# Seven-product pairs: weight sums by two adding transfers and two VectorE additions, attention outputs by way of DRAM

## The chip, the cores and the metric

One NeuronCore of a Trainium2 chip runs the program. The metric is device time in microseconds (us). The engines are TensorE (PE; its weight loads are PEld), VectorE (DVE), ScalarE (ACT), GpSimd (POOL) and SyncE (SP, which here only starts transfers). Transfers between DRAM and SBUF are started from the queues of SP, POOL and ACT. "L145" is line 145 of the kernel.

## The reference

A sequence of 512 tokens with 2048 channels passes through two blocks, all in float32.

- First block, two layers: `h = rmsnorm(x)`, `proj = h @ w_in`; sliding-window attention of 16 heads gives `ya`, latent attention of 8 heads gives `yb`, each times `silu` of its gate; then `x = x + concat(ya, yb) @ w_out`. A final norm follows.
- Second block, one layer: `zin = rmsnorm(x) @ w_in2` is cut into q, k, v, g_attn, u, g_pool, m_attn, m_pool. Stick-breaking attention and a multi-window pool give two outputs, each times `silu` of a gate and then through an up-projection (`w_aup`, `w_pup`); `merged = sigmoid(m_attn) * y_attn + sigmoid(m_pool) * y_pool`, and `x + merged @ w_out2` is normed.

The columns m_attn and m_pool of `zin`, 2048 each, are 32 column tiles of 128. They are what the "pairs" compute.

## The kernel before

**Split matmuls.** Activations lie with channels on the partitions, as tiles of 128 x 512 (channels x tokens). A float32 product is done in three TensorE passes on two rounded halves of each operand: high x high, low x high, high x low. For activations, `split` (L134 ff.) makes the halves: a cast on ACT (names end in `h`), and the difference on DVE (`l`). For weights SP loads a raw tile of 128 x 1024 (`wr`, `w_raw`, L177 to L180), ACT casts `wh` (L209) and DVE subtracts `wl` (L210, recorded as L121). `next_w` makes two weights ahead of the one TensorE works on. There are three buffers for `wh` and for `wl` each; there are three for `wr` and two for `ws`, and a load into a `wr` buffer waits until the `wl` of the tile that it held is done.

**Queues.** Each engine works its own list in order. TensorE's order is as written; a scheduler orders the lists of DVE, ACT, POOL and SP. A load on SP that waits holds up all that stands behind it on SP.

**First block.** Per layer: input products, the side work of the two attentions (stepped forward between matmuls), and at the end the output projection: 16 column tiles j, each a sum over 16 chunks `y[0..15]`, in two halves u of 8 chunks (u=0: y0 to y7, u=1: y8 to y15). The first three tiles run as a group: u=0 for three tiles, then u=1 for three. `yget(c)` splits chunk c. Chunks 0 to 7 are split early (at input product `qa` i, chunk i), 8 to 15 where the output projection first asks for them. All `y` stay in SBUF tiles ("slots", 76 of 128 x 528).

**Pairs.** `run_pair` (L303 ff.) computes two column tiles by seven half-width products in place of eight: 16 pairs, seven products each, each product 8 chunks x 3 passes = 24 matmuls with 256 columns. The results gather in three PSUM tiles z, x, y; ACT copies `m5` from z (L320) and `m1` from x (L322) after the first and second product, and the fourth product, which writes x again, cannot start before `m1`. The weights of the products are, in order: a21+a22, a11, a21+a22+a11, a12, a11+a21, a21+a22+a11+a12, a22 (`pair_steps`, L182 to L204). The sum of products 1, 3 and 6 lives in one tile `ws`, that of product 5 in a `wr` tile. Every addition is an adding transfer on POOL's queue (L192), four in a pair, beside four plain loads by SP. An adding transfer into `ws` must wait until the weight that `ws` held has been split. `pair_out` and `gate_sigmoid` then make two gates `sga` per pair, and SP stores them to DRAM (`sgd`, L1136).

**After the pairs** come 16 rounds of `au` and `pu` (up-projections), which read the 16 tiles `ol` (`o_load`, L1085 to L1088), loaded at the end of the last pair, each split into `oNh` and `oNl`.

Of the kernel before, what the change touches and what calls it, by code (L numbers as in the profile page):

```python
# [35 lines left out]
POOL_W = (2, 4, 8, 16)  # L36

GRP = 3
NSLOT = 76
HN = S // 2  # L40
NSIDE = 3
TP_WAIT = 4000
# [54 lines left out]
def trunk_kernel(ctx, tc, xT, w_in, w_qkv, w_out, w_in2, w_pool, w_aup, w_pup, w_out2, metaT, vec, cst, outT):  # L97
# [22 lines left out]
    def tt(out, a, b, op):  # L120
        nc.vector.tensor_tensor(out, a, b, op)  # L121
# [52 lines left out]
    wq = deque()  # L174
    wready = deque()

    def w_raw(src, n, tag="wr", bufs=3):  # L177
        raw = wp.tile([P, WCOLS], F32, tag=tag, name=tag, bufs=bufs)[:, :n]
        nc.sync.dma_start(raw, src)
        return raw  # L180
# [5 lines left out]
    def pair_steps(a11, a12, a21, a22, n):  # L186


        st = {}

        def add(t, src):
            nc.gpsimd.dma_start(t, src, accum_op=ALU.add)  # L192
            return t

        def s1():
            st["s"] = w_raw(a21, n, "ws", 2)
            return add(st["s"], a22)

        def p11():
            st["r"] = w_raw(a11, n)  # L200
            return st["r"]

        return [s1, p11, lambda: add(st["s"], a11), lambda: w_raw(a12, n), lambda: add(st["r"], a21),
                lambda: add(st["s"], a12), lambda: w_raw(a22, n)]  # L204

    def load_w_split(raw, n):
        hi = wp.tile([P, WCOLS], F32R, tag="wh", name="wh")[:, :n]
# [199 lines left out]
        nc.sync.dma_start(diag_t, cst[:, C_DIAG:C_DIAG + S])  # L407

    xd = [tc.dram_tile([P, NC, S], F32, name=f"xd{i}") for i in range(2)]

    def split_g(x, g, name):
        hi = slot(name + "h", F32R)
# [30 lines left out]
    def swa_pair(i, qps, r, st, nsink, gate, ydst):  # L443
# [78 lines left out]
            nc.scalar.copy(y[on], o[kv][off])  # L522
            tt(y[on], o[kv][on], y[on], ALU.add)
        nc.gpsimd.tensor_tensor(y, y, gate.pop(("a", i)), ALU.mult)
        ydst[8 + i] = y

    def lora_norm(pss, gcol, name, res):

# [73 lines left out]
    def mla_head(h, pr, kr, gate, ydst):  # L602
        hh = h % 2
        qh, ql = pr["qn", hh]
        kh, kl = pr["kn", hh]
        qr = pr["qr", hh]
        krh, krl = kr
        nm = small.tile([P, 4], F32, tag="nm4", name="nm4")
        rs = small.tile([P, 4], F32, tag="rs4", name="rs4")
        pts = []  # L610
        for i in range(NB):
            n = (i + 1) * P
            sc = ps_at("msc")
            qs = slice(i * P, n)
            mm3(sc[:, :n], qh[:, qs], ql[:, qs], kh[:, :n], kl[:, :n], True, False)
            mm2(sc[:, :n], qr[:, qs], krh[:, :n], krl[:, :n], False, True)
            p = slot("mp")
            nc.vector.tensor_tensor_reduce(p[:, :n], sc[:, :n], diag_t[:, S - n:], -MLA_SCALE, 1e38, ALU.add, ALU.min,
                                           nm[:, i:i + 1])
            act(p[:, :n], p[:, :n], AF.Exp, bias=nm[:, i:i + 1], scale=-1.0, accum_out=rs[:, i:i + 1])  # L620
            nc.vector.reciprocal(rs[:, i:i + 1], rs[:, i:i + 1])
            nc.vector.tensor_tensor(p[:, :n], p[:, :n], rs[:, i:i + 1].to_broadcast([P, n]), ALU.mult)
            pts.append(p)
            yield 1200
        yield 2500
        o = ps_at("mo")
        todo = []

        def pv(js, offs, th, tl):
            for j in js:  # L630
                vh, vl = pr["v", j // 2]
                vs = slice((j % 2) * 256 + hh * P, (j % 2) * 256 + hh * P + P)
                cs = slice(offs[j], offs[j] + (NB - j) * P)
                mm3(o[:, j * P:], vh[:, vs], vl[:, vs], th[:, cs], tl[:, cs], j == 0, j == 2)

        for js in ((0,), (1, 3), (2,)):
            tp = ps_at("mtp")
            off = 0
            offs = {}
            for j in js:  # L640
                offs[j] = off
                for i in range(j, NB):
                    transp(tp[:, off:off + P], pts[i][:, j * P:(j + 1) * P])
                    off += P
            th = slot("mTh", F32R)
            tl = slot("mTl", F32R)
            split(tp[:, :off], "", hi=th[:, :off], lo=tl[:, :off])
            if todo:
                pv(*todo.pop())
            todo.append((js, offs, th, tl))  # L650
            yield TP_WAIT
        pv(*todo.pop())
        while ("b", h) not in gate:
            yield 500
        y = slot("yb")
        tt(y, o, gate.pop(("b", h)), ALU.mult)
        ydst[h] = y

    def grouped(w, t0, n):
        for u in range(2):  # L660
# [64 lines left out]
    def layer(lay, h, rd, x_src, x_dst):  # L725
# [12 lines left out]
        y = [None] * NC  # L738
        ys = [None] * NC

        def yget(c):
            if ys[c] is None:
                need(lambda: y[c] is not None)
                ys[c] = split(y[c], f"y{c}")
                y[c] = None
            return ys[c]

# [5 lines left out]
        for kind, i in SEQ1:  # L753
            if kind == "cq":
                if i == 0:
                    pss = run_gemm(2, 8, hget, group=GRP)
                    need(lambda: "r" in rd)
                    start_side(lora_norm([scaled("cq", ps) for ps in pss], V_QA_G + 3 * lay, "cqn", st))
            elif kind == "ckv":
                ckv.append(scaled("ckv"))  # L760
                if i == 1:
                    start_side(lora_norm(ckv, V_KV_G + 2 * lay, "ckvn", st))
            elif kind == "kr":
                kr = split(rope_of(scaled("krf"), "kr"), "krs")
            elif kind == "gb":
                gate["b", i] = gate_silu(run_gemm(2, 8, hget), rd["r"], "gb")
            elif kind == "pa":
                need(lambda: "cqn" in st and "ckvn" in st)
                proj[i] = {}
                mla_proj_a(st["cqn"], st["ckvn"], proj[i])  # L770
                tick()
            elif kind == "pb":
                mla_proj_b(st["cqn"], st["ckvn"], proj[i])
                tick()
            elif kind == "pc":
                pr = proj.pop(i)
                mla_proj_c(st["ckvn"], pr)
                for hh in range(2):
                    start_side(mla_head(2 * i + hh, pr, kr, gate, y), 6000 + 3000 * hh)
            elif kind == "ka":  # L780
                ka = scaled("kaf")
            elif kind == "va":
                start_side(swa_prep(ka, scaled("vaf"), st))
            elif kind == "qa":
                yget(i)
                start_side(swa_pair(i, run_gemm(2, 8, hget), rd["r"], st, nsink, gate, y))
            elif kind == "ga":
                gate["a", i] = gate_silu(run_gemm(2, 8, hget), rd["r"], "ga")

        sq = SumSq("x")  # L790
        if lay == 1:
# [303 lines left out]
    for kind, i in SEQ2:  # L1095
# [32 lines left out]
        elif kind in ("ma", "mp"):  # L1128
# [3 lines left out]
                need(lambda: len(done) == SB)  # L1132
                oo = [None] * (2 * SB)
            at = i + (0 if kind == "ma" else NC)
            for d, t in enumerate(pair_out(run_pair(tset, 8), sr)):
                nc.sync.dma_start(sgd[:, at + d, :], gate_sigmoid(t, "sg"))  # L1136
            if (kind, i) == ("mp", NC - 2):
                X2 = tset = None
                for c in range(2 * SB):
                    oo[c] = o_load(c)  # L1140
        elif kind == "au":
            ya = slot("ym")
            ga = sg_load(i)
# [180 lines left out]
```

## Time and profile before

| | us |
|---|---|
| median of 3 runs | 2794.11 (2786.51 to 2795.55) |
| profiled execution | 2791.94 |
| its span in the trace | 2790.2 |
| PE busy | 2693.0, 97% of the span |
| DVE busy | 1593.4, 57% |
| ACT busy | 1216.4, 44% |
| POOL busy | 459.4, 16% |

PE is busy nearly throughout, and the mean granted clock is 0.989 of full speed. The profile's second part cuts the span into 40 slices of 69.8 us; TensorE's share is 9 tenths or more in all but the first, slices 30 to 35 (2022.8 to 2441.2 us) and the last. A busy PE is not always PE at its full pace, because each record runs from a matmul's start to its modelled end and the records overlap: with 256 columns one takes 0.28 us, and the next starts 0.118 us after it.

### The profile page before, as it was taken

To read this page: it belongs to the slowest core of one execution; us is meant where nothing else is said; L and a number is where in the kernel's file an instruction comes from. 1 tells how busy PE (TensorE), PEld (TensorE's weight loads), DVE (VectorE), ACT (ScalarE), POOL (GpSimd) and SP (SyncE) were. 2 spreads that over 40 slices of the span, in tenths; PEclk is the share of its full clock that TensorE was granted. 3 is DMA by queue.
4 is the path that set the end of the run, shared out by engine and by line. 5 is a ranking of instruction groups with operands and counts; after the bars stand their busy time and mean duration, and the time that the engine had idled before them with its cause. 6 is when DMAs were issued, how large, how long until landed. Compare 5 with 4: busy or idle time off the path is not lost.

```text
span 2790.2 us, 37552 instructions
## 1 busy us (share of the span) xinstructions
PE 2693.0 (97%) x14809; PEld 2321.5 (83%) x14809; DVE 1593.4 (57%) x2399; ACT 1216.4 (44%) x2021; POOL 459.4 (16%) x369
## 2 busy tenths in 40 slices
PE   7999999999999999999999999999988888899997
PEld 5888888888888888888898889898888888688886
DVE  5767567644477667665644444565555555544445
ACT  4445456422345455543334433433345555422322
POOL 4011022111001102124201111112311111011111
PEclk9999999999999999999999999999999999899999
DMA  6222222344322222234422222233388888644334
GB/s 201 75 74 71 77 81 69 111 147 139 97 76 64 78 81 76 76 125 150 134 78 76 79 79 82 70 113 103 94 202 196 198 200 196 183 149 139 125 121 137
DMA packets 107009, 322.39 MB, mean 116 GB/s; under 512 B 11712, under 2 KB 16192, under 8 KB 106832
## 3 DMA queue, kind: packets, MB, share of 16 engines
q1 hardware_dynamic: 97232, 285.78, 32.6%
q0 software_dynamic: 9456, 34.14, 7.0%
q8 instruction: 116, 1.90, 0.3%
q14 instruction: 61, 0.50, 0.1%
q10 hardware_dynamic: 144, 0.07, 0.0%
HBM read 294.78 MB, written 25.17 MB: 115 GB/s over the span
## 4 chain that ended last, share of the span: by engine, by line
PE 77%; DMA 10%; DVE 4%; issue 4%; ACT 4%; POOL 2%; POOLq 0%; SPq 0%; DVEq 0%; ACTq 0%
PE mm L145 55%; DMA ws<-in_w_in 9%; PE mmA L145 5%; PE mmB L145 5%; ACT wh L209 2%; DVE wl L121 1%; PE msc L145 1%; PE qn L145 1%; PE sc L145 1%; PE o L145 1%; PE mo L145 1%; DMA wr<-in_w_in 1%; PE tp L149 1%; ACT sp L128 1%; PE kn L145 1%
## 5 line engine op out<-in xcount | busy, mean ns | idle before, releaser
L209 ACT CAST wh<-wr 128x1024 fp32r<-128x1024 f32 (+2 forms) x448 | 461.6, 1030 | 906.6 <-PE mm L145 616.3
L121 DVE TENSOR_TENSOR wl<-wr,wh 128x1024 fp32r<-128x1024 f32 (+2 forms) x448 | 580.2, 1298 | 316.4 <-ACT wh L209 301.1
L145 PE MATMUL mm<-hh,wh 128*128 128x512 f32 x1024 | 411.7, 402 | 6.6 <-ACT wh L209 6.4
L145 PE MATMUL mm<-hl,wh 128*128 128x512 f32 x1024 | 404.9, 395 | 2.2 <-DVE hl L124 2.2
L145 PE MATMUL mm<-hh,wl 128*128 128x512 f32 x1024 | 405.1, 396 | 0.8 <-DVE wl L121 0.8
L145 PEld LDWEIGHTS mm<-hh,wl 128*128 128x128 f32 x1024 | 193.4, 189 | 47.7 <-DVE wl L121 2.4
L145 PEld LDWEIGHTS mm<-hh,wh 128*128 128x128 f32 x1024 | 194.0, 189 | 42.8 <-ACT wh L209 6.8
L145 PEld LDWEIGHTS mm<-hl,wh 128*128 128x128 f32 x1024 | 194.1, 190 | 39.1 <-DVE hl L124 3.7
L145 PE MATMUL mm<-Xh,wh 128*128 128x512 f32 x384 | 152.6, 398 | 0.0
L145 PE MATMUL mm<-Xh,wl 128*128 128x512 f32 x384 | 151.2, 394 | 0.0
L145 PE MATMUL mm<-Xl,wh 128*128 128x512 f32 x384 | 150.7, 392 | 0.0
L121 DVE TENSOR_TENSOR wl<-ws,wh 128x1024 fp32r<-128x1024 f32 x48 | 59.1, 1231 | 110.5 <-ACT wh L209 109.4
L392 POOL TENSOR_TENSOR gag<-gag,gaa 128x512 f32<-128x512 f32 x24 | 35.5, 1479 | 471.9 <-ACT gaa L128 471.9
L145 PE MATMUL mmA<-Xh,wh 128*128 128x264 f32 x384 | 109.6, 285 | 0.0
L145 PE MATMUL mmB<-Xl,wh 128*128 128x264 f32 x384 | 109.4, 285 | 0.0
L145 PE MATMUL mmB<-Xh,wh 128*128 128x264 f32 x384 | 109.4, 285 | 0.0
L145 PE MATMUL mmA<-Xh,wl 128*128 128x264 f32 x384 | 109.2, 284 | 0.0
L145 PE MATMUL mmA<-Xl,wh 128*128 128x264 f32 x384 | 109.1, 284 | 0.0
L145 PE MATMUL mmB<-Xh,wl 128*128 128x264 f32 x384 | 109.0, 284 | 0.0
L209 ACT CAST wh<-ws 128x1024 fp32r<-128x1024 f32 x48 | 50.3, 1048 | 131.1 <-DMA ws<-in_w_in 104.9
L145 PE MATMUL x<-Xh,wh 128*128 128x256 f32 x256 | 74.7, 292 | 22.4 <-ACT m L322 22.4
L192 POOL DMA_DIRECT2D ws<-in_w_in x48 | 42.6, 968 | 311.9 <-DVE wl L121 220.6
(874 smaller groups left out, 7040.5 us busy)
## 6 DMA issues: line engine op xcount, KB each, us to landing
wr<-in_w_in SPq DMA_DIRECT2D x272, 512.0 KB, 3.7
wr<-in_w_out SPq DMA_DIRECT2D x100, 512.0 KB, 3.6
ws<-in_w_in POOLq DMA_DIRECT2D x48, 512.0 KB, 6.0
ws<-in_w_in SPq DMA_DIRECT2D x16, 512.0 KB, 4.0
xd<-xn SPq DMA_DIRECT2D x32, 256.0 KB, 2.0
wr<-in_w_in POOLq DMA_DIRECT2D x16, 512.0 KB, 8.1
sgd<-sga SPq DMA_DIRECT2D x32, 256.0 KB, 2.5
wr<-in_w_aup SPq DMA_DIRECT2D x16, 512.0 KB, 3.7
```

The source lines that it names most:

```text
L121: nc.vector.tensor_tensor(out, a, b, op)
L128: nc.scalar.activation(out, x, func, bias=bias, scale=scale)
L145: nc.tensor.matmul(out, a, b, start=start, stop=stop, skip_group_check=True)
L149: nc.tensor.transpose(out, x, ident)
L192: nc.gpsimd.dma_start(t, src, accum_op=ALU.add)
L209: nc.scalar.copy(hi, raw)
L392: nc.gpsimd.tensor_tensor(g, g, a, ALU.mult)
```

## The change

1. `pair_steps`: the sum for product 5 (a21+a11) gets a load and an adding transfer of its own (`summed`), so that a11 stays as loaded. The two later additions into `ws` (a11 before product 3, a12 before product 6) are `tensor_tensor` additions in place on VectorE (`plus`). A pair then has five plain loads by SP and two adding transfers by POOL.
2. `wr` has four buffers, the slots are 74.
3. In the first block, chunks 0 to 13 of `y` are stored to DRAM (`yd`) by POOL's queue as soon as they are made, and `yget` loads them again by SP (`yr`) before splitting. Chunks 0 to 7 are asked for at the input products `ga` 4 to 7, two at each, and no longer at `qa`.
4. The gates `sga` are stored by ACT's queue in place of SP's. At the last pair the first eight `ol` loads stand before `pair_out`, the other eight after it.

```diff
--- before.py
+++ after.py
@@ -36,7 +36,7 @@
 POOL_W = (2, 4, 8, 16)
 
 GRP = 3
-NSLOT = 76
+NSLOT = 74
 HN = S // 2
 NSIDE = 3
 TP_WAIT = 4000
@@ -174,7 +174,7 @@
     wq = deque()
     wready = deque()
 
-    def w_raw(src, n, tag="wr", bufs=3):
+    def w_raw(src, n, tag="wr", bufs=4):
         raw = wp.tile([P, WCOLS], F32, tag=tag, name=tag, bufs=bufs)[:, :n]
         nc.sync.dma_start(raw, src)
         return raw
@@ -188,20 +188,22 @@
 
         st = {}
 
-        def add(t, src):
-            nc.gpsimd.dma_start(t, src, accum_op=ALU.add)
+        def raw(name, src, **kw):
+            st[name] = w_raw(src, n, **kw)
+            return st[name]
+
+        def summed(name, src, more, **kw):
+            t = raw(name, src, **kw)
+            nc.gpsimd.dma_start(t, more, accum_op=ALU.add)
             return t
 
-        def s1():
-            st["s"] = w_raw(a21, n, "ws", 2)
-            return add(st["s"], a22)
-
-        def p11():
-            st["r"] = w_raw(a11, n)
-            return st["r"]
-
-        return [s1, p11, lambda: add(st["s"], a11), lambda: w_raw(a12, n), lambda: add(st["r"], a21),
-                lambda: add(st["s"], a12), lambda: w_raw(a22, n)]
+        def plus(name):
+            tt(st["s"], st["s"], st[name], ALU.add)
+            return st["s"]
+
+        return [lambda: summed("s", a21, a22, tag="ws", bufs=2), lambda: raw("a11", a11),
+                lambda: plus("a11"), lambda: raw("a12", a12), lambda: summed("s3", a21, a11),
+                lambda: plus("a12"), lambda: raw("a22", a22)]
 
     def load_w_split(raw, n):
         hi = wp.tile([P, WCOLS], F32R, tag="wh", name="wh")[:, :n]
@@ -407,6 +409,7 @@
         nc.sync.dma_start(diag_t, cst[:, C_DIAG:C_DIAG + S])
 
     xd = [tc.dram_tile([P, NC, S], F32, name=f"xd{i}") for i in range(2)]
+    yd = [tc.dram_tile([P, NC, S], F32, name=f"yd{i}") for i in range(2)]
 
     def split_g(x, g, name):
         hi = slot(name + "h", F32R)
@@ -522,7 +525,7 @@
             nc.scalar.copy(y[on], o[kv][off])
             tt(y[on], o[kv][on], y[on], ALU.add)
         nc.gpsimd.tensor_tensor(y, y, gate.pop(("a", i)), ALU.mult)
-        ydst[8 + i] = y
+        ydst(8 + i, y)
 
     def lora_norm(pss, gcol, name, res):
 
@@ -654,7 +657,7 @@
             yield 500
         y = slot("yb")
         tt(y, o, gate.pop(("b", h)), ALU.mult)
-        ydst[h] = y
+        ydst(h, y)
 
     def grouped(w, t0, n):
         for u in range(2):
@@ -738,10 +741,20 @@
         y = [None] * NC
         ys = [None] * NC
 
+        def ydst(c, t):
+            if c < NC - 2:
+                nc.gpsimd.dma_start(yd[lay][:, c, :], t)
+                t = True
+            y[c] = t
+
         def yget(c):
             if ys[c] is None:
                 need(lambda: y[c] is not None)
-                ys[c] = split(y[c], f"y{c}")
+                t = y[c]
+                if t is True:
+                    t = slot("yr")
+                    nc.sync.dma_start(t, yd[lay][:, c, :])
+                ys[c] = split(t, f"y{c}")
                 y[c] = None
             return ys[c]
 
@@ -776,16 +789,18 @@
                 pr = proj.pop(i)
                 mla_proj_c(st["ckvn"], pr)
                 for hh in range(2):
-                    start_side(mla_head(2 * i + hh, pr, kr, gate, y), 6000 + 3000 * hh)
+                    start_side(mla_head(2 * i + hh, pr, kr, gate, ydst), 6000 + 3000 * hh)
             elif kind == "ka":
                 ka = scaled("kaf")
             elif kind == "va":
                 start_side(swa_prep(ka, scaled("vaf"), st))
             elif kind == "qa":
-                yget(i)
-                start_side(swa_pair(i, run_gemm(2, 8, hget), rd["r"], st, nsink, gate, y))
+                start_side(swa_pair(i, run_gemm(2, 8, hget), rd["r"], st, nsink, gate, ydst))
             elif kind == "ga":
                 gate["a", i] = gate_silu(run_gemm(2, 8, hget), rd["r"], "ga")
+                if i >= 4:
+                    yget(2 * i - 8)
+                    yget(2 * i - 7)
 
         sq = SumSq("x")
         if lay == 1:
@@ -1132,12 +1147,16 @@
                 need(lambda: len(done) == SB)
                 oo = [None] * (2 * SB)
             at = i + (0 if kind == "ma" else NC)
-            for d, t in enumerate(pair_out(run_pair(tset, 8), sr)):
-                nc.sync.dma_start(sgd[:, at + d, :], gate_sigmoid(t, "sg"))
+            c = run_pair(tset, 8)
             if (kind, i) == ("mp", NC - 2):
                 X2 = tset = None
-                for c in range(2 * SB):
-                    oo[c] = o_load(c)
+                for k in range(SB):
+                    oo[k] = o_load(k)
+            for d, t in enumerate(pair_out(c, sr)):
+                nc.scalar.dma_start(sgd[:, at + d, :], gate_sigmoid(t, "sg"))
+            if X2 is None:
+                for k in range(SB, 2 * SB):
+                    oo[k] = o_load(k)
         elif kind == "au":
             ya = slot("ym")
             ga = sg_load(i)
```

TensorE's list of instructions keeps its order. On POOL, in the pair stage, one pair begins at each transfer into a new `ws` tile (the number behind a name tells tiles apart, and is another in each program). Before:

```order
L192 DMA ws_18976<-in_w_in2 128x1024
L192 DMA ws_19454<-in_w_in2 128x1024
L192 DMA ws_19215<-in_w_in2 128x1024
L192 DMA wr_19271<-in_w_in2 128x1024
L192 DMA ws_19215<-in_w_in2 128x1024
L192 DMA ws_19693<-in_w_in2 128x1024
```

The second and third transfer of a pair add to the `ws` that an earlier pair's first transfer added to. After:

```order
L197 DMA ws_18592<-in_w_in2 128x1024
L197 DMA wr_18742<-in_w_in2 128x1024
L197 DMA ws_18833<-in_w_in2 128x1024
L197 DMA wr_18983<-in_w_in2 128x1024
L197 DMA ws_19074<-in_w_in2 128x1024
L197 DMA wr_19224<-in_w_in2 128x1024
```

Four adding transfers per pair have become two; none of them adds to a tile that another one has added to.

On VectorE, in the pair stage, after (`ws_18351` is the sum of one pair, `wr_18469` its a12):

```order
L121 TENSOR_TENSOR c1_18383<-c1_18383,sc2_11821 128x512
L121 TENSOR_TENSOR wl_18441<-ws_18351,wh_18440 128x1024
L121 TENSOR_TENSOR ws_18351<-ws_18351,wr_18469 128x1024
L124 SCALAR_TENSOR_TENSOR sga_18397<-c1_18383,sga_18397 128x512
L121 TENSOR_TENSOR wl_18472<-wr_18469,wh_18471 128x1024
L121 TENSOR_TENSOR wl_18505<-wr_18501,wh_18504 128x1024
L121 TENSOR_TENSOR ab_18499<-m15_18437,y_18406 128x256
L121 TENSOR_TENSOR wl_18534<-ws_18351,wh_18533 128x1024
```

The addition into `ws` stands right behind the `wl` made from the same tile; before, no such row stood on VectorE. The first addition of the same pair, of its a11, stands eight rows above this one.

On SP, at the end of layer 0, where the output projection has begun. Before:

```order
L179 DMA wr_4765<-in_w_out 128x1024
L796 DMA xo_4636<-in_xT 128x512
L179 DMA wr_4827<-in_w_out 128x1024
L179 DMA wr_4857<-in_w_out 128x1024
L179 DMA wr_4923<-in_w_out 128x1024
L179 DMA wr_4953<-in_w_out 128x1024
L804 DMA xd0_92<-xn_4887 128x512
```

Only weights, one old x tile (`xo`) and the store of the new one stand there. After:

```order
L179 DMA wr_4967<-in_w_out 128x1024
L756 DMA yr_4803<-yd0_94 128x512
L756 DMA yr_4812<-yd0_94 128x512
L179 DMA wr_4997<-in_w_out 128x1024
L756 DMA yr_4821<-yd0_94 128x512
L179 DMA wr_5040<-in_w_out 128x1024
L756 DMA yr_4830<-yd0_94 128x512
L756 DMA yr_4839<-yd0_94 128x512
L756 DMA yr_4848<-yd0_94 128x512
L819 DMA xd0_92<-xn_4931 128x512
```

`yr_4803` to `yr_4848` are chunks 8 to 13. Each now stands behind weight loads, which wait for the `wl` of the tile four loads earlier: `wr_4997` for the split of the second weight of u=1, `wr_5040` for that of the third.

On SP, at the end of the last pair. Before:

```order
L179 DMA wr_21628<-in_w_aup 128x1024
L1136 DMA sgd_11629<-sga_21404 128x512
L179 DMA wr_21668<-in_w_pup 128x1024
L1087 DMA ol_21418<-od_11628 128x512
L1136 DMA sgd_11629<-sga_21411 128x512
L1087 DMA ol_21424<-od_11628 128x512
L1087 DMA ol_21430<-od_11628 128x512
L1087 DMA ol_21436<-od_11628 128x512
L1087 DMA ol_21442<-od_11628 128x512
```

The loads `ol` start when the weights of the last pair are on their way, and the store of the second gate stands behind the first of them. After:

```order
L179 DMA wr_21636<-in_w_pup 128x1024
L1102 DMA ol_21514<-od_11714 128x512
L179 DMA wr_21671<-in_w_aup 128x1024
L1102 DMA ol_21520<-od_11714 128x512
L179 DMA wr_21711<-in_w_pup 128x1024
L179 DMA wr_21746<-in_w_aup 128x1024
L1102 DMA ol_21526<-od_11714 128x512
L179 DMA wr_21786<-in_w_pup 128x1024
L1102 DMA ol_21532<-od_11714 128x512
L179 DMA wr_21821<-in_w_aup 128x1024
L1102 DMA ol_21538<-od_11714 128x512
L1102 DMA ol_21544<-od_11714 128x512
```

The first four `ol` loads now stand between weight loads, and no store of a gate stands among them.

## Rows read from the trace of the kernel before

**Rows 1.** Page, part 1: busy us, share of the span, instructions.

```profile
PE 2693.0 (97%) x14809; PEld 2321.5 (83%) x14809; DVE 1593.4 (57%) x2399; ACT 1216.4 (44%) x2021; POOL 459.4 (16%) x369
```

**Rows 2.** Windows, pair stage: stretch, length, busy of PE PEld DVE ACT POOL, clock, DMA, GB/s.

```profile
2162.20:2232.00 69.80, 59.91 (x489) 58.07 (x488) 38.97 (x51) 37.00 (x51) 10.47 (x12) 1.00 0.81 198
```

**Rows 3.** Chain that ended last: shares, then one pair (start, us, what).

```profile
PE mm L145 55%; DMA ws<-in_w_in 9%; PE mmA L145 5%; PE mmB L145 5%; ACT wh L209 2%; DVE wl L121 1%; PE msc L145 1%; PE qn L145 1%; PE sc L145 1%; PE o L145 1%; PE mo L145 1%; DMA wr<-in_w_in 1%; PE tp L149 1%; ACT sp L128 1%; PE kn L145 1%
...
2205.07 7.63 DMA ws<-in_w_in
...
2215.38 5.47 DMA ws<-in_w_in
```

**Rows 4.** Waits of PE: us in total, times, longest.

```profile
PE x L145 <- ACT m L322: 22.4, 14, 2.7
PE y L145 <- ACT wh L209: 12.3, 13, 1.9
PE y L145 <- DVE wl L121: 10.6, 14, 0.8
PE mm L145 <- ACT o0h L136: 8.2, 1, 8.2
```

**Rows 5.** Tile z, all pairs: duration ns min/median/max, first and last start.

```profile
L145 PE MATMUL z<-t12h,wh x128: 274/280/367, 2012.9 to 2376.4; 128*128 128x256 f32 x128
```

**Rows 6.** Timeline of PE, last product of last pair: start, us, what [idle before].

```profile
2391.81 0.28 PE L145 MATMUL y<-t34h,wh 128*128 128x256 f32 x1
...
2394.53 0.28 PE L145 MATMUL y<-t34h,wl 128*128 128x256 f32 x1
2402.97 0.80 PE L145 MATMUL mm<-o0h,wh 128*128 128x512 f32 x1 [8.16 <-ACT o0h L136]
```

**Rows 7.** Page, parts 3 and 6: queue totals; issues (KB each, us to landing).

```profile
q1 hardware_dynamic: 97232, 285.78, 32.6%
q0 software_dynamic: 9456, 34.14, 7.0%
...
wr<-in_w_in POOLq DMA_DIRECT2D x16, 512.0 KB, 8.1
```

**Rows 8.** Timeline of ACT in one pair.

```profile
2217.71 1.03 ACT L209 CAST wh<-wr 128x1024 fp32r<-128x1024 f32 x1
2218.64 0.62 ACT L128 ACTIVATE sga<-sga 128x512 f32<-128x512 f32 x1
2219.18 0.35 ACT L322 COPY m<-x 128x256 f32<-128x256 f32 x1
```

**Rows 9.** Timeline of PE, ACT and DVE, layer 0, output projection to u=1.

```profile
539.40 0.39 PE L145 MATMUL mm<-y8h,wh 128*128 128x512 f32 x1
...
541.49 0.39 PE L145 MATMUL mm<-y11h,wh 128*128 128x512 f32 x1
...
539.37 1.05 ACT L209 CAST wh<-wr 128x1024 fp32r<-128x1024 f32 x1 [1.89 <-PE mm L145]
...
513.65 2.38 DVE L121 TENSOR_TENSOR wl<-wr,wh 128x1024 fp32r<-128x1024 f32 x1
...
540.46 1.23 DVE L121 TENSOR_TENSOR wl<-wr,wh 128x1024 fp32r<-128x1024 f32 x1 [0.25 <-ACT wh L209]
```

**Rows 10.** DMA issues of 256 KB: KB each, median us to landing.

```profile
xo<-in_xT SPq DMA_DIRECT2D x16, 256.0 KB, 2.9
...
ol<-od SPq DMA_DIRECT2D x16, 256.0 KB, 4.6
```

**Rows 11.** Timeline of PE: a wait of the pair stage.

```profile
2046.02 0.39 PE L145 MATMUL y<-t12h,wh 128*128 128x256 f32 x1 [1.79 <-ACT wh L209]
```

**Rows 12.** Windows, behind that wait.

```profile
2048.00:2052.00 4.00, 4.00 (x21) 4.00 (x20) 2.74 (x3) 3.63 (x7) 0.38 (x1) 0.50 0.79 116
```

**Rows 13.** Timeline of SP, end of the pair stage.

```profile
2401.46 4.29 SPq L1087 DMA_DIRECT2D ol<-od  x9
...
2414.28 2.75 SPq L1087 DMA_DIRECT2D ol<-od  x6
```

## Prediction before the run

> **What bounds the kernel now.** I read the page first. TensorE is busy 97% of the span [rows 1], so only two things can pay: a stretch in which it waits, and one in which its records are spread wider than its pace. The windows show one large stretch of that kind, the pair stage. There the busy time of PE is 59.9 of 69.8 us at the full clock, the other engines are at most 56% busy, and the DMA engines are at 0.81 [rows 2]. The chain that ended last says what the stage runs at: `DMA ws` has 9% of the whole span, and inside a pair it is two adding transfers on one `ws` tile, 7.63 and 5.47 us, with a cast and a subtraction between [rows 3]. TensorE itself sees this as three small waits in most pairs: for the copy `m1`, for the cast `wh` and for `wl`, 22.4 + 12.3 + 10.6 = 45.3 us [rows 4]. Behind the last pair comes one wait of 8.16 us for the first `ol` tile [rows 6].
>
> **The pair stage, what it could take.** It runs from 2012.9 [rows 5] to the end of the last product, 2394.53 + 0.28 = 2394.81 [rows 6]: 381.9 us, 23.9 per pair. The last product shows the pace without waits: first and last of its 24 matmuls are 2.72 us apart, 0.118 us each, 2.84 for a product, 19.9 for seven, 318 for 16 pairs. The difference is 64 us: the 45.3 us of waits; the end of each modelled record, which hides 0.16 us of each of the 41 waits (7 us); and matmuls at half clock behind the longer waits, as after the one of 1.79 us, where the next 4 us have a granted clock of 0.50 (1.2 GHz) [rows 11, 12], for the rest of about 12.
>
> **What the edit does to it.** *Transfers.* The software queue has 7.0% of 16 engines' span for 64 adding transfers: 195 us, 3.05 each. The hardware queue has 32.6% for 285.78 MB: 1.67 us for each load of 0.524 MB [rows 7]. A pair before holds the engines for 0.81 of 23.9 us, 19.4 us. After, two adding transfers go and one load comes: 19.4 - 6.1 + 1.7 = 15.0 us, which fits into 19.9 (0.75). The two that stay have no chain: the first sum is started as soon as its tile is free, a pair and a half ahead, and the sum a11+a21 about 9 us into the pair before its use. With the longest row of its kind, 8.1 us to landing [rows 7], behind a load, it lands near 20, and its cast is due at about 27.
>
> *VectorE.* Two additions of 128 x 1024 per pair. No such addition is in the trace; the subtraction that makes `wl` has the same size and two SBUF inputs, and takes 1.23 us at one place and 2.38 at another, where POOL computes beside it [rows 9]. These are the bounds; I take 1.23, since in the pair stage POOL only issues transfers. VectorE is busy 38.97 of 69.8 [rows 2], times 23.9, 13.3 us per pair, and will be at 13.3 + 2.5 = 15.8 of 19.9. The second addition waits for the load of a12, and the next `wl` and two gate steps are queued behind it, so a late a12 would reach TensorE by way of that `wl`. But the weights are made two ahead: laid out step by step with the durations of [rows 8, 9], each `wl` ends 1.4 to 4 us before TensorE asks for it. At 2.4 us per addition the least of these margins is used up, and a pair takes about 1 us longer, 16 us in all.
>
> *ScalarE.* It gets the two stores of gates per pair: at 0.48 us per issue, as SP's nine in 4.29 us [rows 13], 1 us on 12.7 of 19.9 (37.00 of 69.8 [rows 2], times 23.9). More important is the order there: `m1` is late today because the cast of `wh` before it is late (2217.71, then 0.62 of a gate, then the copy at 2219.18 [rows 8]). That cast is late because all of them queue up behind the cast of `ws`, which waits for the transfer. With the transfer early `m1` comes about 6.7 us into the pair and is due at 8.5.
>
> So the stage becomes bound by TensorE at 19.9 us a pair. I leave 3 us for the entry (first pair, half clock) and take **-61** of the possible 64; bounds -40 (the 22.4 us for `m1` stay) and -64.
>
> **Behind the pairs.** Today SP starts nine `ol` loads only at 2401.46, held by a store of a gate that waits for its activation, and the last six at 2414.28, held by a weight load [rows 13]. After, four stand ahead of the last pair's end, no store is among them, but eight of sixteen are behind a weight load still. The 8.16 us for o0 go; the matmuls then meet o5 to o15 as they land, one by one. I take **-6**, bounds 0 and -10.
>
> **The first block: attention outputs by way of DRAM.** 28 stores and 28 loads of 256 KB. The bytes (14.7 MB) are 47 us of all DMA engines, of which the span has 60% free (32.6 and 7.0% used [rows 7]); I cost them at nothing. POOL's stores wait for the chunk itself, and what stands behind them on POOL are gate products that are wanted later still. Where they are not hidden is the point at which the output projection asks for chunks 8 to 15. Before, all eight are split straight from SBUF, and TensorE passes from y8 to y11 at its pace [rows 9]. After, chunks 8 to 13 must be loaded, and SP's list puts y11, y12, y13 behind the weight load `wr_5040`. That load takes the buffer of the third u=1 weight, whose cast can start only when TensorE is done with the third tile of u=0. In the trace that cast is at 539.37 and its `wl` ends at 541.69, while TensorE starts y8 at 539.40 and wants y11 at 541.49 [rows 9]. Then: two issues to 542.1, 2.9 us to landing as for `xo` [rows 10] is 545.0, 0.62 us for the cast and the low half a little later, some 545.6. TensorE stands still from 541.5 for 4.1, and for another 0.4 at the low half: 4.5 us. y12 and y13 are right behind and cost little more. With 4.6 us to landing, as `ol` [rows 10], it would be 6.2. A wait of that size is followed by half clock as in [rows 11, 12]; four microseconds at 1.2 GHz give back 2 us of work too few. So 6.5 per layer, and the order is the same in layer 1: **+13**, bounds 0 (loads land earlier than the list suggests) and +20.
>
> The Trainium skill says the same of the clock (TensorE: Matmul & The Clock Gate, "What's actually happening"): an idle TensorE falls to 4/8 of its clock and must be busy again for a while before it is given back. By it the two stalls cost 13 as above, without it 9; the trace, with 0.50 behind a wait of 1.79 us, is on its side.
>
> The rest: 74 slots for 76, with eight or more `y` tiles fewer in SBUF, nothing. The start of the program has one more weight buffer and the POOL queue holds the first adding transfer behind a load: 0, bounds -2 and +2.
>
> **Sum.** 2791.94 - 61 - 6 + 13 = 2738 for a run like the profiled one. The median of the runs is 2.2 above it: **2740**.
>
> **The rivals.**
> (a) *The pair stage stays half bound.* If the wait for `m1` stays (its cast still behind gate work on ScalarE, now with two stores more), or the DMA engines cannot be driven past the 0.81 they have, or the additions take 2.4 us, a pair takes about 21.4 in place of 19.9: -40 in place of -61, 2761. For it: `m1` has only 1.8 us of slack, and ACT's and DVE's lists are in order. Against: 15.0 us of transfers in 19.9, no engine over 80%. The Trainium skill warns here (DMA: Bandwidth & Descriptors, "Issuing engines are not separate DMA queues"): transfers from SP, ACT and POOL run on the same 16 engines and interleave, so that moving the gate stores to ACT's queue relieves no engine. By it the stores stay in the 15.0 us, where I have them, and an addition that remains still shares its engines with the loads.
> (b) *The reload costs nothing.* If the loads of y10 to y13 find their place before TensorE comes to them, the 13 go: 2727. Against it stands the order of SP's list, which is fixed.
> (c) *Slower.* Each reload is a load, a cast and a subtraction in a chain, 2.9 us [rows 10] and twice about 0.62 [rows 8], 4.1 us. If SP, held by weight loads at each of them, puts every one of the 28 on TensorE's path, they cost 115 us: 2740 - 13 + 115 = 2842. It decides from about 2.7 us per reload, where 76 us eat the 67 gained and the 8.4 of the bound below. Against: chunks 0 to 7 are asked for at `ga` 4 to 7, several products ahead of their use.
> (d) *The sum moves nothing*, since the pair stage is bound by something that the chain hides, all transfers together for example: -10 there, -6, +13: about 2791. For it speaks the 0.81 at only 198 GB/s [rows 2]; against it, that [rows 7] price an adding transfer at 3.05 us and a load at 1.67, and half of the dear kind go.
>
> **How the numbers follow.** Forecast 2740 (2728 to 2752): 0.58. (a) 0.19, (b) 0.14, (c) 0.04, (d) 0.05. Tell-apart is about 0.3%, 8.4 us, since the three runs lie 9 us apart. Faster by more: forecast, (a), (b) and a little of (d): 0.92; same: the rest of (d), 0.04; slower: (c), 0.04. The range reaches from (b) into (a): 2722 to 2767.
>
> **What would show it.** Windows of the pair stage: PE busy near 69.8 of 69.8, clock 1.00, DMA share near 0.75, z's first starts spread over about 300 us for 16 pairs. In the waits of PE: `m`, `wh` and `wl` under pairs gone, the line for o0 small, and new lines at the output projections, on `y10l`, `y11h` or `y11l`, twice, some 4 us each, with half clock behind them. Wrong it would be made by waits for a `ws` or `wr` transfer in the pair stage, by waits on `y0` to `y7`, or by stalls of SP on the free slots.

## The result

The changed kernel takes 2761.75 us (median of 4 runs, 2760.89 to 2763.09), the kernel before, beside it, 2791.96. The ratio is 0.9894, 95% interval 0.9876 to 0.9912: faster by about 1.1%. The forecast was 2740 with a range of 2722 to 2767. The profiled execution has a span of 2759.8 us, 30.4 less than before.

The total hides two large terms of opposite sign. TensorE runs the same list of matmuls in both kernels, so each one can be found in both traces and its starts compared. That difference, after minus before, as it builds up along the program:

| up to (time in the trace before) | difference, us | of this stretch |
|---|---|---|
| first column sum, 49 | -1.4 | -1.4 |
| first `mm<-y0h` of layer 0, 520.7 | +4.0 | +5.4 |
| output projection of layer 0, 700 | +19.1 | +15.1 |
| first `mm<-y0h` of layer 1, 1196 | +24.3 | +5.2 |
| output projection of layer 1, 1376 | +36.2 | +11.9 |
| first product of the pairs, 2012.9 | +36.8 | +0.6 |
| last product of the pairs, 2394.5 | -26.4 | -63.2 |
| second up-projection, 2425.5 | -30.8 | -4.4 |

The pair stage gave 63.2 us, the first block took 38.2 of them back. The first `mm<-y0h` runs before the last matmuls of the attention, so the two rows of the output projections hold losses of two kinds: up to the first `mm<-y8h` +6.0 and +4.8 us, and at u=1, from there to the last `mm<-y15l` of the group of three tiles, +8.4 and +7.7 us. So u=1 lost 16.1 us, and the attention ahead of it some 20.

**Pair stage.** The windows of the kernel after (columns as in [rows 2]):

```profile
2094.00:2163.80 69.80, 69.80 (x593) 69.80 (x592) 53.78 (x65) 42.79 (x58) 5.81 (x7) 1.00 0.77 210
2163.80:2233.60 69.80, 69.80 (x593) 69.80 (x592) 56.09 (x70) 45.08 (x63) 6.26 (x8) 1.00 0.81 216
```

The first product of all pairs, and the timeline of PE at the end of the last one, which answer to [rows 5, 6]:

```profile
L145 PE MATMUL z<-t12h,wh x128: 276/283/287, 2049.7 to 2350.9; 128*128 128x256 f32 x128
```

```profile
2368.15 0.28 PE L145 MATMUL y<-t34h,wl 128*128 128x256 f32 x1
2368.27 0.39 PE L145 MATMUL mm<-o0h,wh 128*128 128x512 f32 x1
```

TensorE is busy for all of 69.80 us, at the full clock, 593 matmuls where it was 489. The stage takes 2368.4 - 2049.7 = 318.7 us, and the first matmul of the next stage follows without a wait. The DMA engines are at 0.77 to 0.81, where [rows 2] have 0.81, and TensorE does not wait for them: that 0.81 was no sign that transfers were at their limit. The addition on VectorE, in the timeline of one pair, right behind the `wl` that is made from the same tile:

```profile
2211.32 1.22 DVE L121 TENSOR_TENSOR wl<-ws,wh 128x1024 fp32r<-128x1024 f32 x1
2212.58 1.23 DVE L121 TENSOR_TENSOR ws<-ws,wr 128x1024 f32<-128x1024 f32 x1
```

**First block.** The waits of TensorE, which answer to [rows 4]:

```profile
PE csum L145 <- ACT csh L136: 10.5, 1, 10.5
PE mm L145 <- ACT y11h L136: 7.1, 2, 3.6
PE o L145 <- DVE pTl L121: 6.7, 8, 1.0
PE mm L145 <- ACT wh L211: 6.5, 1, 6.5
PE o L145 <- ACT pTh L136: 4.8, 2, 2.5
PE zA L145 <- DVE sufl L121: 4.7, 8, 0.6
PE mm L145 <- ACT o8h L136: 4.5, 1, 4.5
PE csum L145 <- ACT oq L128: 2.1, 1, 2.1
PE mm L145 <- DVE y10l L121: 1.5, 2, 0.8
```

All lines of the pairs (`x`, `y` in [rows 4]) are gone. New are `y11h` and `y10l`, twice each, the forecast stall; and new are `pTl` and `pTh`, waits of the attention itself, which no step of the prediction had. (The wait for `csh` at the start is longer, 10.5 for 7.7 us, but it begins earlier; that stretch is 1.4 us shorter.) SP, ACT and PE around y11 in layer 0 (start, us, what, idle before and what ended it):

```profile
551.76 0.33 SPq L179 DMA_DIRECT2D wr<-in_w_out  x1
552.20 1.32 SPq L756 DMA_DIRECT2D yr<-yd  x3
...
556.10 0.62 ACT L136 CAST y11h<-yr 128x512 fp32r<-128x512 f32 x1 [5.10 <-DMA yr<-yd]
...
552.39 0.50 PE L145 MATMUL mm<-y10l,wh 128*128 128x512 f32 x1 [0.84 <-DVE y10l L121]
556.77 0.79 PE L145 MATMUL mm<-y11h,wh 128*128 128x512 f32 x1 [3.65 <-ACT y11h L136]
```

The load of y11 is issued at once after the weight load, and TensorE stands still for 3.65 us. The windows behind that wait, and behind the other new wait (below):

```profile
557.00:560.00 3.00, 3.00 (x7) 2.09 (x8) 2.96 (x5) 2.06 (x4) 0.00 (x0) 0.50 0.00 0
535.00:540.00 5.00, 5.00 (x15) 3.90 (x14) 1.23 (x1) 1.04 (x1) 0.00 (x0) 0.57 0.04 7
```

The granted clock is 0.50 (1.2 GHz) behind it, and still 0.50 in a window up to 563.2. And this is the wait on `pTh`, some 20 us earlier, in the timelines of SP, ACT and PE:

```profile
527.02 0.33 SPq L179 DMA_DIRECT2D wr<-in_w_out  x1
527.47 0.36 SPq L756 DMA_DIRECT2D yr<-yd  x1
...
531.32 0.62 ACT L136 CAST y7h<-yr 128x512 fp32r<-128x512 f32 x1 [2.33 <-DMA yr<-yd]
531.85 0.85 ACT L136 CAST pTh<-tp 128x512 fp32r<-128x512 f32 x2
...
532.48 0.58 PE L145 MATMUL o<-pTh,vz 128*128 128x256 f32 x1 [2.31 <-ACT pTh L136]
```

`pTh` is the last attention pair's, and needs nothing of y7. But ACT works its list in order, the cast of y7 stands in front, and that cast waits for a load which SP issues late, behind a weight load that waits. So a chunk that TensorE comes to only after `pTh` (y7h is used at 535.4) holds up work that it wants at 530.2.

The waits on `pTl`, of about 1 us, come without a late load. In an earlier attention pair VectorE has the low half of y3 to make ahead of `ya` and `pTl`:

```profile
489.43 0.69 DVE L121 TENSOR_TENSOR y3l<-yr,y3h 128x512 fp32r<-128x512 f32 x1
490.03 1.40 DVE L121 TENSOR_TENSOR ya<-o,ya 64x512 f32<-64x512 f32 x2
491.46 1.29 DVE L121 TENSOR_TENSOR pTl<-tp,pTh 128x512 fp32r<-128x512 f32 x2
...
492.21 0.39 PE L145 MATMUL o<-pTl,vz 128*128 128x256 f32 x1 [1.00 <-DVE pTl L121]
```

### The profile page after: what moved, and what is told of

Its sections match the earlier page's. It is cut to its first block, busy times and chain, and to the rows that moved or that the text cites. A ratio compares the mean times of both kernels' runs of the same rounds, so it can differ in the third digit from the quotient of the medians.

```text
span 2759.8 us, 37622 instructions
## 1 busy us (share of the span) xinstructions
PE 2689.3 (97%) x14809; PEld 2316.5 (84%) x14809; DVE 1629.6 (59%) x2431; ACT 1219.9 (44%) x2021; POOL 434.0 (16%) x365
## 4 chain that ended last, share of the span: by engine, by line
PE 51%; issue 2%; DVE 2%; ACT 1%; POOL 1%; DMA 1%; SPq 0%; DVEq 0%; POOLq 0%; ACTq 0%
PE mm L145 27%; PE mmA L145 5%; PE y L145 5%; PE mmB L145 5%; PE x L145 3%; PE z L145 3%; ACT sp L128 1%; PE so L145 1%; POOL suf L979 0%; DVE out L1221 0%; DMA ol<-od 0%; POOL suf L978 0%; PE pw L145 0%; DVE sufl L121 0%; DMA yr<-yd 0%
## 5 line engine op out<-in xcount | busy, mean ns | idle before, releaser
L121 DVE TENSOR_TENSOR wl<-wr,wh 128x1024 fp32r<-128x1024 f32 (+2 forms) x448 | 573.6, 1282 | 349.6 <-ACT wh L211 334.5
L145 PEld LDWEIGHTS mm<-hl,wh 128*128 128x128 f32 x1024 | 193.4, 189 | 38.2 <-DVE hl L124 2.5
L379 POOL TENSOR_TENSOR xq<-xq 128x512 f32<-128x512 f32 x30 | 53.0, 1768 | 259.4 <-ACT xq L128 259.4
L130 ACT ACTIVATE p<-p,nm 128x256 f32<-128x256 f32 (+1 forms) x128 | 60.7, 475 | 57.3 <-DVE nm L480 56.1
L145 PEld LDWEIGHTS mm<-Xh,wl 128*128 128x128 f32 x384 | 72.1, 188 | 16.6
L145 PEld LDWEIGHTS mm<-Xh,wh 128*128 128x128 f32 x384 | 72.2, 188 | 15.2
```

Source lines behind the costliest of these rows:

```text
L130: nc.scalar.activation(out, x, func, bias=bias, scale=scale, accum_out=accum_out)
L145: nc.tensor.matmul(out, a, b, start=start, stop=stop, skip_group_check=True)
L379: nc.gpsimd.tensor_tensor(self.acc, self.acc, q, ALU.add)
```

## The experiments

The theory: the new sums take the chain of adding transfers off the pair stage and give its 63 us; the 38 us lost in the first block come from where the reloads and splits of y stand on the lists of SP, ACT and DVE, in two places: about 16 us at u=1 of the two output projections, and about 20 in the attention, where y0 to y7 are split since the change. Rivals: the transfers themselves, POOL's stores or the two slots fewer cost it; the fourth buffer or the gate stores gave the gain. Ratios are to the kernel before, with 95% intervals.

**e1_no_detour**: all y stay in SBUF, chunk i is split at `qa` i.

```diff
-            if c < NC - 2:
+            if c < 0:
...
             elif kind == "qa":
+                yget(i)
...
-                if i >= 4:
-                    yget(2 * i - 8)
-                    yget(2 * i - 7)
```

> The changed kernel with all chunks of y kept in SBUF and split where the kernel before splits them (chunk i at product qa i); weight sums, four wr buffers, 74 slots, gate stores on ACT and the ol loads stay as changed. Theory 1 (the first block loses its 38 us by the reloads: about 16 at u=1 of the two output projections, the rest by splits of y0 to y7 that stand before attention steps on ACT and DVE): the whole loss goes, 2762 - 38 = 2724 us, no waits on y11h, pTh or pTl. Rival 2 (the loss is of two slots fewer, or of the fourth wr buffer's other order on SP): it stays, 2755 to 2762.

Measured: 2724.58 us (2724.00 to 2726.11), 0.9760 (0.9744 to 0.9777). The whole loss goes; at the first product of the pairs the difference to the kernel before is +0.4 us, where it was +36.8. So the detour and the moved splits cost 36.4 us; the rest of the 38.2 is the 1.4 us gained at the start, which are gone at 463 us in this version too. Two slots fewer and the fourth buffer cost nothing there. This version beats both kernels, by 37 and by 67 us.

**e2_reload_early_split**: the detour stays, chunks 0 to 7 are asked for at `qa` i.

```diff
             elif kind == "qa":
+                yget(i)
...
-                if i >= 4:
-                    yget(2 * i - 8)
-                    yget(2 * i - 7)
```

> The changed kernel, only that chunk i (0 to 7) is asked for, reloaded and split at product qa i and not two by two at ga 4 to 7. Theory 1: the waits on pTl and pTh (some 20 us with the half clock behind them) go, those on y10 and y11 at u=1 stay: 2742 us. Rival 3 (a reload in the attention part costs wherever it stands, since POOL's stores or SP's order hold it): 2755 or more, with waits on pTh or pTl at qa in their place.

Measured: 2738.01 us (2737.07 to 2738.59), 0.9807 (0.9792 to 0.9821). 23.7 us go, 4 more than expected. Its waits of TensorE:

```profile
PE mm L145 <- ACT wh L211: 7.3, 1, 7.3
PE mm L145 <- ACT y11h L136: 7.2, 2, 3.7
PE zA L145 <- DVE sufl L121: 4.6, 8, 0.6
PE mm L145 <- ACT o8h L136: 4.5, 1, 4.5
PE csum L145 <- ACT oq L128: 1.8, 1, 1.8
PE mm L145 <- DVE y10l L121: 1.4, 2, 0.7
```

`pTl` and `pTh` are gone, `y11h` and `y10l` are as they were. At the first product of the pairs the difference is +15.6 us, 15.1 of it at u=1 of the two layers: this is the cost of the forecast stall with its half clock.

**e3_keep_8_to_13**: only chunks 0 to 7 go by DRAM, split at `ga` as changed.

```diff
-            if c < NC - 2:
+            if c < 8:
```

> The changed kernel, only that chunks 8 to 13 stay in SBUF; 0 to 7 go by DRAM and are split at ga 4 to 7 as changed. Theory 1: the waits on y10l and y11h and the half clock behind them go, 16 us: 2746 us; the waits on pTl and pTh stay. If the two losses were one (a late reload of y7 makes the later ones late), more than 16 would go: 2735 or less.

Measured: 2743.37 us (2742.47 to 2745.23), 0.9827 (0.9813 to 0.9842). 18.4 us go; `y11h` is gone from the waits, and these stay:

```profile
PE o L145 <- DVE pTl L121: 6.7, 8, 1.0
...
PE o L145 <- ACT pTh L136: 4.9, 2, 2.4
```

e2 and e3 take away 23.7 and 18.4 us, together 42; e1, which takes both, 37. The two places are separate up to 5 us. No run splits y0 to y7 at `ga` out of SBUF, so how much of the loss in the attention comes from the place of the splits and how much from the late loads is not told apart by a run; the trace above shows both.

**e4_old_sums**: `pair_steps` of the kernel before, all else as changed (the helpers `add`, `s1` and `p11` come back with it).

```diff
...
-        return [lambda: summed("s", a21, a22, tag="ws", bufs=2), lambda: raw("a11", a11),
-                lambda: plus("a11"), lambda: raw("a12", a12), lambda: summed("s3", a21, a11),
-                lambda: plus("a12"), lambda: raw("a22", a22)]
+        return [s1, p11, lambda: add(st["s"], a11), lambda: w_raw(a12, n), lambda: add(st["r"], a21),
+                lambda: add(st["s"], a12), lambda: w_raw(a22, n)]
```

> The changed kernel with the weight sums of the kernel before (four adding transfers, chained on ws), all else as changed, the fourth wr buffer too. Theory 1 (the chain of adding transfers set the pair stage's pace, and its removal gave the 63 us there): the pair stage is back at 23.5 to 24 us a pair, 2822 us. Rival 4 (the fourth wr buffer or the gate stores' move to ACT's queue gave a good part): 2790 to 2805.

Measured: 2821.47 us (2820.49 to 2828.77), 1.0112 (1.0096 to 1.0127). Most of the gain is of the sums: the pair stage takes only 5.8 us less here than before the change, so that 57.4 of the 63.2 us are theirs. Which other part gave the 5.8 is not shown; e10 below speaks against the gate stores. The pairs' lines are back in its waits, as in [rows 4]:

```profile
PE x L145 <- ACT m L322: 22.6, 16, 1.6
PE y L145 <- ACT wh L209: 10.8, 14, 2.1
```

Without the new sums the rest of the change costs 29 us.

**e5_preload**: as e2, and the loads of chunks 8 to 13 are asked for behind `ga` 7.

```diff
+                if i == 7:
+                    for c in range(8, NC - 2):
+                        ypre(c)
...
+        def ypre(c):
+            need(lambda: y[c] is not None)
+            if y[c] is True:
+                t = slot("yr")
+                nc.sync.dma_start(t, yd[lay][:, c, :])
+                y[c] = t
```

> The changed kernel with the same 28 stores and 28 loads of y, but chunks 0 to 7 split at products qa 0 to 7, and the loads of chunks 8 to 13 put on SP's list right behind ga 7, ahead of the weight loads that wait. Theory 1 (the transfers themselves are hidden; what costs is where their loads stand on SP's list and where the casts behind them stand on ACT's): no waits on y10, y11, pTh or pTl, and the time of the kernel without the detour, 2725 us (2722 to 2729). Rival 5 (the bytes, POOL's stores or the late landing of any load cost by themselves): 2733 or more, with waits on y chunks.

Measured: 2725.21 us (2724.63 to 2725.96), 0.9766 (0.9752 to 0.9781), the time of e1 within a microsecond, with all 56 transfers of y still made. So the transfers themselves, POOL's stores among them, cost nothing; the whole loss was their place on the lists. To SP's list this does (`yr_4668` to `yr_4678` are chunks 8 to 13, `wr_5040` the weight load that y11 stood behind):

```order
L179 DMA wr_4871<-in_w_out 128x1024
L754 DMA yr_4668<-yd0_94 128x512
L754 DMA yr_4670<-yd0_94 128x512
L754 DMA yr_4672<-yd0_94 128x512
L754 DMA yr_4674<-yd0_94 128x512
L754 DMA yr_4676<-yd0_94 128x512
L754 DMA yr_4678<-yd0_94 128x512
L819 DMA xo_4680<-in_xT 128x512
L179 DMA wr_4901<-in_w_out 128x1024
L179 DMA wr_4967<-in_w_out 128x1024
L179 DMA wr_4997<-in_w_out 128x1024
L179 DMA wr_5040<-in_w_out 128x1024
```

**e6_sums_alone**: the kernel before with the new `pair_steps` and nothing else (three `wr` buffers, 76 slots).

```diff
...
+            tt(st["s"], st["s"], st[name], ALU.add)
...
+                lambda: plus("a11"), lambda: raw("a12", a12), lambda: summed("s3", a21, a11),
+                lambda: plus("a12"), lambda: raw("a22", a22)]
```

> The kernel before with the new weight sums alone: three wr buffers, 76 slots, gate stores on SP, ol loads after the last pair, no detour. Theory 1, if three wr buffers are enough: the pair stage takes 319 us and nothing else changes, 2794 - 63 = 2731. Rival 6 (five loads and the tile of a21+a11 need the fourth buffer): the pair stage keeps waits for wr tiles, 340 us or more, 2750 or more.

Measured: 2733.08 us (2727.59 to 2741.57), 0.9797 (0.9775 to 0.9818), near the 2731 expected. The runs spread over 14 us, and the profiled one, on their slow end with a span of 2739.8, still has waits in the pairs, where the stage gives 52.3 of 63 us:

```profile
PE x L145 <- ACT m L324: 7.9, 6, 2.4
```

So three buffers nearly do; whether the fourth is what makes the time steady was not tried apart.

**e7_ws_by_transfers**: e1 with the two later additions into `ws` by adding transfers, a21+a11 still in its own tile.

```diff
-            tt(st["s"], st["s"], st[name], ALU.add)
+            nc.gpsimd.dma_start(st["s"], a11 if name == "a11" else a12, accum_op=ALU.add)
```

> The kernel without the detour (2724.6 us), but both later additions into ws by adding transfers again; a21+a11 keeps a tile of its own, so that a pair has five loads and three... four adding transfers as before the change (one for a21+a22, two into ws, one for a21+a11). Theory 1 (the chain on ws sets the pace): the pair stage is back at about 23.5 us a pair, 2782 us. Rival 7 (the chain of a21 behind a11's split was the limit): it stays near 320, 2725 to 2735.

Measured: 2834.50 us (2834.19 to 2834.87), 1.0158 (1.0143 to 1.0173): the direction of the theory, 52 us beyond its number. The waits, a window of the pair stage, and a link of the chain:

```profile
PE y L145 <- ACT wh L211: 61.6, 14, 5.4
```

```profile
2170.00:2240.00 70.00, 54.39 (x405) 52.68 (x404) 30.79 (x40) 29.52 (x43) 7.83 (x9) 0.87 0.73 183
```

```profile
2224.17 11.76 DMA ws<-in_w_in
```

The link that took 7.63 us in [rows 3] takes 11.76 here, where five plain loads stand beside four adding transfers; that this is why was not tried apart. The pair stage takes 45 us more than before the change, a part of it at half clock: the granted clock of the window is 0.87. Its DMA share is 0.73, less than the 0.77 to 0.81 at which the changed kernel passes without a wait, so it is not the use of the DMA engines that holds TensorE here. Four adding transfers per pair without the chain were not tried.

**e8_dve_only**: e1 with a21 added into the tile of a11, as before; the two additions stay on VectorE.

```diff
+        def into(name, more):
+            nc.gpsimd.dma_start(st[name], more, accum_op=ALU.add)
+            return st[name]
...
-                lambda: plus("a11"), lambda: raw("a12", a12), lambda: summed("s3", a21, a11),
+                lambda: plus("a11"), lambda: raw("a12", a12), lambda: into("a11", a21),
```

> The kernel without the detour (2724.6 us), with the two additions on VectorE, but a21 added into the tile of a11 as in the kernel before, in place of a load and a tile of its own: four loads and two adding transfers per pair. Theory 1: the adding transfer starts behind the first addition on VectorE, some 2 us before the pair begins, lands 8 us later and is wanted at 11: the pair stage stays at 319 us, 2725 us (to 2730). Rival 7 (that tile of its own was needed): 2740 or more, with waits for wh or m1 in the pairs.

Measured: 2730.62 us (2729.81 to 2731.84), 0.9786 (0.9770 to 0.9803): 6 us above e1 and just above the 2730 allowed, from one wait of 5.7 us for `m` in one pair. Of the change's three edits on the sums the two additions on VectorE carry the gain; the tile for a21+a11 is worth a few microseconds.

**e9_ol_on_pool**: e1 with all `ol` loads ahead of the last pair's gate work, the last eight on POOL's queue.

```diff
-                for k in range(SB):
+                for k in range(2 * SB):
...
-        nc.sync.dma_start(t, od[:, c, :])
+        (nc.sync if c < SB else nc.gpsimd).dma_start(t, od[:, c, :])
```

> The kernel without the detour (2724.6 us), with all sixteen ol loads asked for ahead of the last pair's gate work, the last eight of them on POOL's queue, which has nothing else to do there, in place of SP's, where they stand behind a weight load. Theory 1 (behind the pairs the gain was smaller than forecast since o8 to o15 are still held by that weight load and by the gate work ahead of the cast of o8 on ACT): the wait of 4.3 us on o8h goes, and with it the half clock, 2718 to 2721 us. Rival 8 (the casts and subtractions of sixteen tiles on ACT and DVE set the pace there): the waits move to other o tiles, 2723 to 2727.

Measured: 2724.88 us (2724.68 to 2725.95), 0.9759 (0.9745 to 0.9772), no change to e1. Theory 1 fell; the time is the one that rival 8 gives, but its longest wait is not for an `o` tile. The wait for o8 goes, and a longer one comes, for VectorE's `c`. PE and DVE:

```profile
2352.24 0.76 PE L145 MATMUL mm<-o8h,wh 128*128 128x512 f32 x1 [7.21 <-DVE c L121]
...
2351.08 0.68 DVE L121 TENSOR_TENSOR o15l<-ol,o15h 128x512 fp32r<-128x512 f32 x1
2351.68 0.42 DVE L121 TENSOR_TENSOR c<-x,sc 128x256 f32<-128x256 f32 x1
```

`c` reads the last pair's results out of PSUM. Now it stands behind all sixteen splits, and the matmul that waits is the first of the next product, whose result goes to a tile of the same PSUM pool.

**e10_gates_on_sp**: e1 with the gate stores on SP.

```diff
-                nc.scalar.dma_start(sgd[:, at + d, :], gate_sigmoid(t, "sg"))
+                nc.sync.dma_start(sgd[:, at + d, :], gate_sigmoid(t, "sg"))
```

> The kernel without the detour (2724.6 us), with the gate stores on SP's queue as in the kernel before. Theory 1 (SP's stores were no limit in the pair stage once the weight sums are not): the pair stage stays at 319 us and the time within 3 us of 2724.6; behind the pairs a store that waits for its gate holds the last ol loads, 1 to 3 us more. Rival 4 (their move to ACT was needed to reach the pace): waits for wr tiles in the pairs, 2735 or more.

Measured: 2724.29 us (2723.87 to 2724.88), 0.9756 (0.9743 to 0.9769): the move to ACT's queue gave nothing.

## Why the prediction was right, and where it was wrong

- *Pair stage, -61: right*, -63.2, for the reason given (e4, e7). Its parts too: VectorE's addition 1.23 us as taken, no wait left, DMA share 0.77 to 0.81 where 0.75 was expected. One link of the chain was left out: of the 9% that it has of the span, a part is the plain load into the next `ws` tile, which stands in the chain of before ahead of the 7.63 us of [rows 3]:

```profile
2199.85 4.12 DMA ws<-in_w_in
```

- *Behind the pairs, -6: -4.4.* The wait for o0 went, a wait of 4.5 us for o8 took its place. That a weight load holds the last eight `ol` was not all of it: freed from it, the program takes as long, since a wait set by VectorE's order comes in its place (e9).
- *Reload at u=1, +13: +16.1*, and 15.1 in e2, with the waits where they were foreseen: in layer 0 y11 3.65 us and y10 0.84, together the 4.5 forecast. What was too small is the half clock behind them, taken as 2 us per layer: the 8.4 us of layer 0 leave some 3.9 beside these waits. The granted clock was 0.50 behind the wait of 3.65 us. The Trainium skill (TensorE: Matmul & The Clock Gate, "What's actually happening") has an idle TensorE fall to 4/8 of its clock; the trace agrees, with that 0.50.
- *The wrong step:* "28 stores and 28 loads ... I cost them at nothing" outside u=1, and in rival (c) "chunks 0 to 7 are asked for at `ga` 4 to 7, several products ahead of their use". Their own use was not what was delayed. Their splits were moved from `qa`, where e2 shows no wait on account of them, to `ga`, between the steps of the attention, and there they stand in front of a `pTh`, `pTl` or `ya` that TensorE wants sooner. That term was taken as 0 and measured about 20 us: some 20 by places in the trace, 21.2 between this kernel and e2 at the first product of the pairs (36.8 - 15.6), 23.7 between their whole times. TensorE waits for no `y0` to `y7`, which would have been a sign of being wrong; the loss showed in waits that the prediction had not listed.
- So 2762 came out where rival (a) had put 2761, and (a) was not what happened: no pair was half bound. It lies outside the 2728 to 2752 of the forecast proper, and inside the whole range only because that reached into (a): that the time as a whole came out in the range was luck, since the sum had nothing for the term that was missed. A time that fits a rival does not show the rival; the windows of the stage do.
- Rival (b), a reload that costs nothing, is refuted for this kernel, and true for e5: at u=1 it was a matter of SP's list, as the prediction said.

## What to carry to other kernels

When an operation moves to another place in the program, look at what stands behind it on each in-order engine there, not only at whether its own result is in time: a cast that waits for a load holds all that comes after it, as that of y7 held `pTh` for 2.31 us. Loads that are to be hidden belong ahead of the queue entries that wait for buffers. And a sum that chains transfers on one tile is limited by their latency one after the other, here at DMA shares of 0.73 to 0.81 (e7 and before); one engine addition of 1.23 us took the place of a link of 5 to 8.

## What the hardware showed that was not expected

An adding transfer is slow to land even where half as many run. The issues of the changed kernel (KB each, median us to landing), which answer to those of [rows 7]:

```profile
wr<-in_w_in SPq DMA_DIRECT2D x288, 512.0 KB, 3.6
...
ws<-in_w_in POOLq DMA_DIRECT2D x16, 512.0 KB, 8.0
```

It takes more than twice the time of a plain load, and no less than the 6.0 us (into `ws`) and 8.1 us (into `wr`) of the kernel before. It is not a fixed time: in e8, with one plain load less per pair, the medians are 6.5 and 5.3 us. And the DMA share of 0.81 at 198 GB/s in the pairs before, which rival (a) read as near a limit, was reached again at 216 GB/s without a wait, with half of the adding transfers gone.
